# Seven block products for eight in the gate and up projections of the first token group, with smaller mixer buffers, an output projection fed by token range, and a shorter last reduction

## The chip, the cores and the metric

One core of a Trainium2 chip runs the whole kernel. The metric is the time of one execution on the device in microseconds (us). The engines have these names in all views: PE (matrix products, on TensorE), PEld (its weight loads), DVE (vector), ACT (scalar), POOL (GpSimd), SP (which here only issues DMAs). A DMA is issued by an engine's own instruction and runs on 16 DMA engines.

## The reference

One layer of an encoder over 1024 prompt tokens and 32 tokens of a running stream, all in fp32:

```python
h = x * (1 + sc1) + sh1                                   # conditioning from c @ w_ada
mq, mk, mv, mo, mi, mf, fq, fk, fv, ff, gu, gv = split(h @ w_in)
hm = mlstm(...)      # matrix memory, 4 heads       -> 256 columns
hf = fox(...)        # attention with forgetting, 8 heads -> 512 columns
hg = gmlp(...)       # spatial gate                 -> 256 columns
mix = concat([hm, hf, hg]) @ w_o
x = layer_norm(ALPHA * x + (1 + g1) * mix)
h = x * (1 + sc2) + sh2
y = (silu(h @ w_gate) * (h @ w_up)) @ w_down             # D_MODEL 1024, D_FF 2816
x = layer_norm(ALPHA * x + (1 + g2) * y)
```

## The kernel before

**Tiling.** Activations lie transposed, features on the 128 partitions, tokens along the free axis. The 1056 tokens are two groups: group 0 has 512, group 1 has 544 (two ranges of 272). D_FF is 22 tiles of 128 columns; a "tile j" below is the pair of gate and up columns number j, whose weights are `w_gu[j]`, 128 rows by 2048 (8 k-blocks of 128 for gate, 8 for up). Every fp32 product takes three passes of TensorE (`gemm`, L119 to L121): the weight and the activation are split into a rounded part (`whi`, `ah`) and a remainder (`wlo`, `al`), and the passes are hi by high, hi by low and lo by high. The split of a weight is one cast by ACT (L107) and one subtraction by DVE (L108), each on 1024 columns.

**Order of the program.** (1) Conditioning and the first projection; (2) the input projections, woven with the mixers of group 0; (3) `wo_mix(0)` loads the mixers' output of group 0 from DRAM (`dmix`) and splits it into the operand `ah`/`al`, `wo(0)` makes the output projection, range by range of 256 tokens, `ln1` normalizes; (4) the last projections of group 1; (5) the mixers of group 1 (`mixers`), at the same time the gate and up products (`up`) and the down products (`down`) of group 0: I call this the mixer stage, from about 470 to 900 us; (6) `wo(1)` and its normalization, and the rest of group 0's products; (7) the gate, up and down products of group 1; (8) the last normalization (`ln2`) and the stores.

**What sets the order.** The code is written through a tile framework whose scheduler places the instructions of each engine by priority and its own costs; the code's `weave` and `issue_after` are hints. Each engine then runs its own list strictly in order. Buffers are taken from pools of a fixed count, so an instruction also waits until the reader of an older buffer is done.

**The block scheme.** Group 1's tiles 3 to 20 are not made by `up` but by `sup`: of gate and up, each with two halves of 512 rows of k, and two token ranges, eight block products would be needed; `sup` forms sums of weight blocks and sums of operand blocks and makes seven products of 4 k-blocks by 272 tokens (84 matmuls). The operand's sums come once from `sup_operand`. Of the weights' sums, two come from DRAM: `sums()` stores a block of `w_gu` twice into `dp[j]` (a DMA of SP, L90), and a DMA of POOL (L1078) then adds two other blocks to it; two more are made by DVE out of the loaded blocks (L1132, L1133). Group 0 uses `up` for all 22 tiles: 2 times 8 k-blocks by 3 passes, 48 matmuls of 128x512.

**Last step.** `ln_sum` adds each finished row block m into `zs` (POOL, L899) and its square into `qs` (DVE, L901); `ln_stats` sums over the partitions by one product each with a matrix of 1/1024 (L908, L910).

## Time and profile before

| | |
|---|---|
| median of 3 runs | 1407.58 us (1405.99 to 1407.97) |
| the profiled execution | 1411.39 us, of which 1409.6 us are the span of its instructions |
| granted TensorE clock, mean over the span | 0.986 of full speed |
| PE busy | 1346.1 us (95%), 9437 matmuls |
| DVE / ACT / POOL busy | 999.4 (71%) / 656.3 (47%) / 261.1 us (19%) |
| DMA | 233.06 MB, a mean of 165 GB/s |

The page is read so: the shares are means over all stages, so the stages are looked at one by one, in rows that give for a stretch of time the busy time of each engine with its instruction count, the granted clock (1.00 is full speed), the DMA engines' busy share and the GB/s they moved. Rows of the timeline give start, duration, engine, line of the kernel, operation, and in brackets the idle time before it with what ended it. Matmuls are pipelined, so that the time a product costs is the distance from start to start, not its own duration.

### The profile page before, as it was taken

To read this page: it belongs to the slowest core of one execution; us is meant where nothing else is said; L and a number is where in the kernel's file an instruction comes from. 1 tells how busy PE (TensorE), PEld (TensorE's weight loads), DVE (VectorE), ACT (ScalarE), POOL (GpSimd) and SP (SyncE) were. 2 spreads that over 40 slices of the span, in tenths; PEclk is the share of its full clock that TensorE was granted. 3 is DMA by queue.
4 is the path that set the end of the run, shared out by engine and by line. 5 is a ranking of instruction groups with operands and counts; after the bars stand their busy time and mean duration, and the time that the engine had idled before them with its cause. 6 is when DMAs were issued, how large, how long until landed. Compare 5 with 4: busy or idle time off the path is not lost.

```text
span 1409.6 us, 25370 instructions
## 1 busy us (share of the span) xinstructions
PE 1346.1 (95%) x9437; PEld 1229.6 (87%) x9437; DVE 999.4 (71%) x2145; ACT 656.3 (47%) x1309; POOL 261.1 (19%) x297
## 2 busy tenths in 40 slices
PE   6999999999989899999999999999989999999995
PEld 4899989899979778888888878898989999999985
DVE  5548655578679657677767857577967887777666
ACT  3323244444445444545545354435744564636344
POOL 0103200042246500000000120073600000022031
PEclk9999999999999999999999999999999999999997
DMA  9754677575664864444444344675675768544221
GB/s 377 255 197 133 186 231 245 175 210 162 191 200 152 222 201 125 131 144 117 135 121 131 90 115 79 192 182 149 180 199 150 211 165 227 155 127 128 86 73 64
DMA packets 132915, 233.06 MB, mean 165 GB/s; under 512 B 22180, under 2 KB 79148, under 8 KB 129720
## 3 DMA queue, kind: packets, MB, share of 16 engines
q1 hardware_dynamic: 127624, 221.48, 51.3%
q0 software_dynamic: 5168, 9.96, 4.7%
q8 instruction: 74, 1.21, 0.4%
q14 instruction: 49, 0.40, 0.1%
HBM read 197.50 MB, written 53.81 MB: 178 GB/s over the span
## 4 chain that ended last, share of the span: by engine, by line
PE 73%; DMA 10%; DVE 8%; ACT 3%; issue 3%; POOL 2%; SPq 1%; ACTq 0%; DVEq 0%; POOLq 0%
PE up_g L121 4%; PE up_g L119 4%; PE up_g L120 4%; PE dn_g L119 4%; PE dn_g L120 4%; PE dn_g L121 4%; PE tm_g L312 2%; PE tm_g L313 2%; PE tm_g L311 2%; PE fm_g L119 2%; PE sup_g L119 2%; PE sup_g L121 2%; PE sup_g L120 2%; PE fm_g L120 2%; PE fox_t L773 2%
## 5 line engine op out<-in xcount | busy, mean ns | idle before, releaser
L119 PE MATMUL up_g<-mlstm_ah,up_whi 128*128 128x512 f32 x328 | 131.9, 403 | 3.7 <-DVE fm_qkl L396 2.5
L121 PE MATMUL up_g<-mlstm_ah,up_wlo 128*128 128x512 f32 x328 | 131.0, 399 | 0.0
L120 PE MATMUL up_g<-mlstm_al,up_whi 128*128 128x512 f32 x328 | 130.9, 399 | 0.0
L119 PE MATMUL fm_g<-start_h1h,fm_whi 128*128 128x256 f32 (+2 forms) x344 | 101.6, 303 | 9.5 <-DVE fm_qkl L396 4.8
L313 PE MATMUL tm_g<-tm_whi,start_h1l 128*128 128x256 f32 (+1 forms) x384 | 110.4, 288 | 0.0
L311 PE MATMUL tm_g<-tm_whi,start_h1h 128*128 128x256 f32 (+1 forms) x384 | 110.4, 289 | 0.0
L312 PE MATMUL tm_g<-tm_wlo,start_h1h 128*128 128x256 f32 (+1 forms) x384 | 110.1, 287 | 0.0
L120 PE MATMUL fm_g<-start_h1l,fm_whi 128*128 128x256 f32 (+2 forms) x344 | 101.5, 295 | 0.0
L121 PE MATMUL fm_g<-start_h1h,fm_wlo 128*128 128x256 f32 (+2 forms) x344 | 100.5, 293 | 0.0
L1126 ACT CAST sup_whi<-sup_raw 128x1024 fp32r<-128x1024 f32 x54 | 56.5, 1048 | 78.3 <-PE dn_u L120 37.2
L107 ACT CAST up_whi<-up_raw 128x1024 fp32r<-128x1024 f32 x50 | 52.3, 1046 | 64.2 <-PE up_g L120 29.5
L108 DVE TENSOR_TENSOR up_wlo<-up_raw,up_whi 128x1024 fp32r<-128x1024 f32 x50 | 63.2, 1264 | 25.8 <-ACT up_whi L107 24.9
L1127 DVE TENSOR_TENSOR sup_wlo<-sup_raw,sup_whi 128x1024 fp32r<-128x1024 f32 x54 | 68.6, 1275 | 15.4 <-ACT sup_whi L1126 15.1
L747 ACT ACTIVATE fox_p<-fox_s,fox_fmx 128x384 f32<-128x384 f32 (+2 forms) x96 | 55.3, 580 | 49.6 <-DVE fox_fmx L740 43.2
L119 PEld LDWEIGHTS fm_g<-start_h1h,fm_whi 128*128 128x128 f32 x344 | 65.2, 191 | 14.9 <-ACT start_h1h L232 8.2
L119 PEld LDWEIGHTS up_g<-mlstm_ah,up_whi 128*128 128x128 f32 x328 | 62.0, 189 | 17.6 <-DVE fm_qkl L396 3.0
L119 PE MATMUL dn_g<-up_acth,dn_whi 128*128 128x512 f32 (+2 forms) x200 | 73.7, 369 | 0.8 <-DVE mlstm_z L982 0.8
L120 PEld LDWEIGHTS up_g<-mlstm_al,up_whi 128*128 128x128 f32 x328 | 62.1, 189 | 14.1 <-issue 0.8
L121 PEld LDWEIGHTS up_g<-mlstm_ah,up_wlo 128*128 128x128 f32 x328 | 62.1, 189 | 13.9 <-issue 0.4
L312 PEld LDWEIGHTS tm_g<-tm_wlo,start_h1h 128*128 128x128 f32 x384 | 73.1, 190 | 0.7 <-issue 0.4
L313 PEld LDWEIGHTS tm_g<-tm_whi,start_h1l 128*128 128x128 f32 x384 | 73.0, 190 | 0.6 <-issue 0.4
L311 PEld LDWEIGHTS tm_g<-tm_whi,start_h1h 128*128 128x128 f32 x384 | 72.9, 190 | 0.8 <-issue 0.4
(618 smaller groups left out, 4561.2 us busy)
## 6 DMA issues: line engine op xcount, KB each, us to landing
up_raw<-w_gu SPq DMA_DIRECT2D x50, 512.0 KB
ada_late<-w_ada SPq DMA_DIRECT2D x16, 1024.0 KB
dn_raw<-w_dn SPq DMA_DIRECT2D x28, 512.0 KB
wo_raw<-w_o SPq DMA_DIRECT2D x24, 512.0 KB
sup_raw<-w_gu SPq DMA_DIRECT2D x20, 512.0 KB
start_dp<-w_gu SPq DMA_DIRECT2D x19, 512.0 KB
start_dp<-w_gu POOLq DMA_DIRECT2D x19, 512.0 KB, 7.6
sup_raw<-start_dp SPq DMA_DIRECT2D x18, 512.0 KB
```

Of the source, the lines that this page charges most:

```text
L107: nc.scalar.copy(hi[:, :w], raw[:, :w])
L108: (eng or nc.vector).tensor_tensor(lo[:, :w], raw[:, :w], f(hi[:, :w]), ALU.subtract)
L119: nc.tensor.matmul(ps, hi, xh(k), start=start and k == 0, stop=False, skip_group_check=more)
L120: nc.tensor.matmul(ps, hi, xl(k), start=False, stop=False, skip_group_check=more)
L121: nc.tensor.matmul(ps, lo, xh(k), start=False, stop=stop and k == n - 1, skip_group_check=more)
L311: nc.tensor.matmul(ps[:, :ncol], xh, hi, start=k == 0, stop=False)
L312: nc.tensor.matmul(ps[:, :ncol], xh, lo, start=False, stop=False)
L313: nc.tensor.matmul(ps[:, :ncol], xl, hi, start=False, stop=k == 7)
L747: nc.scalar.activation(pr[:, lo:hi], banks[x][:, :hi - lo], AF.Exp, bias=m, scale=-1.0 if hi == n else 1.0, accum_out=sums[:, x:x + 1])
L773: nc.tensor.transpose(ps[:, at + (y - first) * P:at + (y - first + 1) * P], probs[y][:, b * P:(b + 1) * P], self.ident)
L1126: nc.scalar.copy(h, x)
L1127: tt(l, x, f(h), ALU.subtract)
```

## The change

1. **Group 0, tiles 3 to 18, by `sup`.** `sup` gets the group as an argument; for group 0 it makes 84 matmuls of 128x256 where `up` made 48 of 128x512. `sup_operand0` builds the operand's sums from the residual `z` when tile 3 comes up: 8 ACT activations of 512 columns, then subtractions and splits by DVE and ACT, through one `sil` buffer. One sum overwrites a quarter of the operand in place, so `corner_store` saves that quarter in DRAM and `corner_load` brings it back after tile 18. For group 0 the two additions of weight blocks are made by POOL instead of DVE.
2. **`sums()` earlier.** The 19 stores and the 19 accumulating DMAs go from 900 to 1250 us to the mixer stage, two of them before it.
3. **Buffers.** The mixers' pool for group 1 has one `p` buffer and one `pth` buffer less, the mLSTM steps share buffers, `sil` has one buffer for two, and the row constants are split in two tiles.
4. **Softmax scaling.** `FP` is a table of which engine divides by the softmax sum in the attention of each group: for group 1 ACT does it instead of DVE (L755).
5. **`wo_mix(0)` by token range.** The eight loads of range 0 go ahead of those of range 1, and the first loads go ahead of the load of the residual.
6. **Conditioning units 20 to 23** go from the first tiles of group 0 to the projection loop before.
7. **Last reduction.** In the last half of group 1 the last two row blocks are not added to `zs` and `qs` but summed by TensorE as further products (`direct`, `more`); `ln2_end` normalizes in pieces of 4, 2, 1 and 1 blocks.

```diff
-FP = (0, 0)
+FP = (0, 1)
+MX1 = (1, 1, 1, 1, 3, 2)
+SJ0 = 3
+SE0 = 18
+SIL = 1
...
+    def sup_operand0(self):
...
+        (th, tl), (uh, ul) = self.T0
+        for k in range(4):
+            x, y = self.t(self.p2, [P, 544], F32, "sil", SIL)[:, :512], ys[k]
+            for q, o in ((k, x), (k + 4, y)):
+                nc.scalar.activation(o, self.z[0][:, q], AF.Identity, bias=self.modcol("sh2", q)[0],
+                                     scale=self.modcol("sc2", q)[0])
+            tt(y[:, b], y[:, b], x[:, b], ALU.subtract)
+            tt(x[:, b], x[:, a], x[:, b], ALU.subtract)
+            stt(x[:, a], x[:, a], -1.0, y[:, b], ALU.mult, ALU.subtract)
+            stt(y[:, a], x[:, a], -1.0, y[:, a], ALU.mult, ALU.subtract)
+            nc.scalar.copy(th[:, k], x)
+            tt(tl[:, k], x, f(th[:, k]), ALU.subtract)
+            nc.scalar.copy(uh[:, k], y[:, b])
+            tt(ul[:, k], y[:, b], f(uh[:, k]), ALU.subtract)
+        h, l = self.whole
+        for k in range(4):
+            nc.scalar.copy(h[:, k, b], ys[k][:, a])
+            tt(l[:, k, b], ys[k][:, a], f(h[:, k, b]), ALU.subtract)
...
-    def sup(self, j, act, pool):
+    def sup(self, c, j, act, pool):
...
-        tt(raw[0][:, lo], raw[0][:, lo], raw[1][:, hi], ALU.add)
-        tt(raw[0][:, hi], raw[0][:, hi], raw[0][:, lo], ALU.add)
+        add = (nc.vector if c else nc.gpsimd).tensor_tensor
+        add(raw[0][:, lo], raw[0][:, lo], raw[1][:, hi], ALU.add)
+        add(raw[0][:, hi], raw[0][:, hi], raw[0][:, lo], ALU.add)
...
+        if m in st.get("direct", ()):
+            st["more"].append((z[:, m, sl], sq))
+            return
...
-        self.wo_mix(0, self.KORDER[:6])
+        self.wo_mix(0, self.KORDER[:6], MM[0][:1])
...
-        self.wo_mix(0, self.KORDER[6:])
+        self.wo_mix(0, self.KORDER[6:], MM[0][:1])
+        self.wo_mix(0, self.KORDER, MM[0][1:])
...
-                weave(self.up(0, j, act, pa, FC[0]))
-                if j < 4:
-                    self.ada(20 + j, pa, "late", 1, self.pg, "g")
+                if j and self.nsum <= FF:
+                    self.sums(self.lastraw)
+                if j < SJ0:
+                    weave(self.up(0, j, act, pa, FC[0]))
+                else:
+                    if j == SJ0:
+                        weave(self.sup_operand0())
+                    weave(self.sup(0, j, act, pa))
```

How the change moves instructions is seen at three places in the engines' lists. In these rows stand the line, the operation, output and inputs with their buffer numbers, and the shape of the output; lines of the changed kernel are some higher (L123 to L125 are its three passes, L90 is its load, L94 its store).

SP, ahead of `wo(0)`. The operand of range 0 needs eight loads `wo_tmp`, one for each k-block. Before, six of them (4286 to 4306) are followed by six of range 1 (4310 to 4330), and only then by the last two of range 0 (5271, 5275):

```order
L90 DMA o_kT<-fm_qkr_5187 64x272
L90 DMA start_dqh_57<-fm_qkh_5226 128x272
L90 DMA start_dql_58<-fm_qkl_5227 128x272
L90 DMA o_kT<-fm_qkr_5228 64x272
L86 DMA wo_tmp_4318<-start_dmix_32_88 128x256
L86 DMA wo_tmp_4322<-start_dmix_32_88 128x256
L86 DMA wo_tmp_4326<-start_dmix_32_88 128x256
L86 DMA wo_tmp_4330<-start_dmix_32_88 128x256
L90 DMA start_dqh_57<-fm_qkh_5260 128x272
L90 DMA start_dql_58<-fm_qkl_5261 128x272
L90 DMA o_kT<-fm_qkr_5262 64x272
L86 DMA wo_tmp_5271<-start_dmix_32_88 128x256
```

Now the last two of range 0 (5242, 5246) come as the seventh and eighth load, ahead of all of range 1 (5250 and on):

```order
L94 DMA start_dqh_57<-fm_qkh_5122 128x272
L94 DMA start_dql_58<-fm_qkl_5123 128x272
L94 DMA o_kT<-fm_qkr_5124 64x272
L94 DMA start_dqh_57<-fm_qkh_5156 128x272
L94 DMA start_dql_58<-fm_qkl_5157 128x272
L94 DMA o_kT<-fm_qkr_5158 64x272
L94 DMA start_dqh_57<-fm_qkh_5197 128x272
L90 DMA wo_tmp_5242<-start_dmix_33_89 128x256
L90 DMA wo_tmp_5246<-start_dmix_33_89 128x256
L90 DMA wo_tmp_5250<-start_dmix_33_89 128x256
```

Six loads and the stores of two more projections no longer stand between the sixth and the seventh load of range 0.

PE, the first tiles of group 0 in the mixer stage. Before, the 24 products of a gate half and the 24 of an up half stand in one run each:

```order
L119 MATMUL up_g_8307<-mlstm_ah_4284,up_whi_8297 128x512
L120 MATMUL up_g_8307<-mlstm_al_4285,up_whi_8297 128x512
L121 MATMUL up_g_8307<-mlstm_ah_4284,up_wlo_8298 128x512
L119 MATMUL up_g_8332<-mlstm_ah_4284,up_whi_8303 128x512
L120 MATMUL up_g_8332<-mlstm_al_4285,up_whi_8303 128x512
```

Now the first block tile (bank `sup_g_8671` and `sup_g_8715`; `up_th`, `up_tl`, `up_uh`, `up_ul` are the operand's sums) is spread k-block by k-block between down products and attention:

```order
L871 MATMUL foxs_o_6514<-foxs_pth_6511,start_vs_158 64x32
L745 MATMUL fox_s_6547<-fox_k_1178_6532,fox_q_1179_6533 128x384
L745 MATMUL fox_s_6551<-fox_k_1178_6532,fox_q_1179_6533 128x256
L124 MATMUL sup_g_8671<-up_tl_8585,sup_whi_8658 128x256
L125 MATMUL sup_g_8671<-up_th_8584,sup_wlo_8659 128x256
L124 MATMUL sup_g_8715<-up_ul_8587,sup_whi_8662 128x256
L125 MATMUL sup_g_8715<-up_uh_8586,sup_wlo_8663 128x256
L123 MATMUL dn_g_8795<-up_acth_8362,dn_whi_8780 128x512
L124 MATMUL dn_g_8795<-up_actl_8363,dn_whi_8780 128x512
```

The products of tile 3 that need the operand's sums now stand ahead of down products that don't need them, in a list that PE runs in order.

POOL in the mixer stage. Before, it has three short instructions for each mLSTM step and nothing else:

```order
L554 MEMSET mlstm_mqb_6660 128x512
L559 MEMSET mlstm_mv_1230_6664 128x4
L570 TENSOR_TENSOR mlstm_mo_6667<-mlstm_mo_6667,start_rowp_175 128x256
L554 MEMSET mlstm_mqb_7098 128x512
L559 MEMSET mlstm_mv_1356_7102 128x4
L570 TENSOR_TENSOR mlstm_mo_7105<-mlstm_mo_7105,start_rowp_175 128x256
```

Now the two additions of each block tile (L1187, L1188) and the accumulating DMAs (L1091) stand in the same list:

```order
L574 TENSOR_TENSOR mlstm_mo_6746<-mlstm_mo_6746,start_rowp_176 128x256
L1187 TENSOR_TENSOR sup_raw_8646<-sup_raw_8646,sup_raw_8647 128x512
L1188 TENSOR_TENSOR sup_raw_8646<-sup_raw_8646 128x512
L1091 DMA start_dp_19_75<-w_gu 256x1x512
L1187 TENSOR_TENSOR sup_raw_8894<-sup_raw_8894,sup_raw_8895 128x512
L1188 TENSOR_TENSOR sup_raw_8894<-sup_raw_8894 128x512
L1091 DMA start_dp_20_76<-w_gu 256x1x512
L1091 DMA start_dp_21_77<-w_gu 256x1x512
L1187 TENSOR_TENSOR sup_raw_9030<-sup_raw_9030,sup_raw_9031 128x512
L1188 TENSOR_TENSOR sup_raw_9030<-sup_raw_9030 128x512
L558 MEMSET mlstm_mqb_7172 128x512
```

An accumulating DMA waits for its store to land, and additions of later tiles and memsets of later mLSTM steps are queued behind it.

181 lines of the change are left out of this document (124 added, 57 removed).

## The prediction

> **What bounds the kernel now.** I read the page first, then the busy times by stage, because the change adds work to three engines in one stage and takes some from a fourth.
>
> ```profile
> span 1409.6 us, 25370 instructions
> PE 1346.1 (95%) x9437; PEld 1229.6 (87%) x9437; DVE 999.4 (71%) x2145; ACT 656.3 (47%) x1309; POOL 261.1 (19%) x297
> q0 software_dynamic: 5168, 9.96, 4.7%
> 380.00:440.00 60.00, 52.85 (x412) 51.45 (x412) 47.85 (x66) 30.86 (x54) 34.84 (x31) 0.97 0.65 201
> 500.00:900.00 400.00, 397.75 (x2089) 328.56 (x2088) 274.16 (x565) 187.82 (x379) 17.51 (x26) 1.00 0.46 126
> 1000.00:1050.00 50.00, 46.43 (x356) 45.73 (x356) 41.08 (x76) 27.91 (x58) 13.54 (x15) 0.97 0.79 213
> 1050.00:1340.00 290.00, 289.15 (x2292) 287.96 (x2291) 224.83 (x398) 150.30 (x246) 29.51 (x26) 1.00 0.57 157
> ```
>
> The last four rows are stretches: length, then PE, PEld, DVE, ACT and POOL busy, the granted clock, the DMA share and GB/s. In the mixer stage (500 to 900) PE is busy 99.4% while DVE is at 69%. In group 1's block stage (1050 to 1340) DVE is at 78% and PE still at 99.7%. PE sets the pace in both, so a matmul less is time less as long as the others keep up. At 380 to 440, around the output projection of group 0, PE loses 7 us of 60.
>
> **Term 1: the products.** What a matmul costs is the distance of starts.
>
> ```profile
> 400.10 0.28 PE L119 MATMUL wo_g<-mlstm_ah,wo_whi 128*128 128x256 f32 x1
> 401.87 0.29 PE L119 MATMUL wo_g<-mlstm_ah,wo_whi 128*128 128x256 f32 x1
> 702.20 0.39 PE L121 MATMUL dn_g<-up_acth,dn_wlo 128*128 128x512 f32 x1
> 706.38 0.40 PE L121 MATMUL dn_g<-up_acth,dn_wlo 128*128 128x512 f32 x1
> ```
>
> These are first and last of two runs without a gap: 15 intervals of a 256-column product in 1.77 us, 0.118 each, and 18 intervals of a 512-column one in 4.18 us, 0.232 each. A tile of group 0 goes from 48 x 0.232 = 11.14 us to 84 x 0.118 = 9.91, a gain of 1.23; over 16 tiles **-20 us** (19.7, and 20.3 with unrounded spacings).
>
> A page speaks against this: the Trainium skill, "TensorE: Matmul & The Clock Gate", section "Back-to-back issue gap", has sustained spacings of 81 ns for 128 columns and 131 ns for 512. By a line between them, an estimate, 256 columns take 98 ns, a tile goes from 6.3 to 8.2 us, and 16 tiles cost 31 us more. This trace disagrees (118 and 232 ns); the same section's formula for an isolated product, columns / 2.4 + 2.5 ns, is what the rows follow.
>
> **Term 2: DVE, ACT and POOL in the mixer stage.** Durations, from the mixer stage and from group 1's block stage:
>
> ```profile
> L108 DVE TENSOR_TENSOR up_wlo<-up_raw,up_whi 128x1024 fp32r<-128x1024 f32 x38 | 46.8, 1232 | 21.6 <-ACT up_whi L107 20.7
> L1060 DVE TENSOR_TENSOR up_actl<-up_sil,up_acth 128x512 fp32r<-128x512 f32 x19 | 13.0, 684 | 0.9 <-ACT up_acth L1059 0.9
> L755 DVE TENSOR_SCALAR fox_p<-fox_p,fox_fsm 128x1024 f32<-128x1024 f32 x8 | 6.0, 753 | 0.2
> L755 DVE TENSOR_SCALAR fox_p<-fox_p,fox_fsm 128x640 f32<-128x640 f32 x8 | 4.4, 550 | 0.2
> L1127 DVE TENSOR_TENSOR sup_wlo<-sup_raw,sup_whi 128x1024 fp32r<-128x1024 f32 x50 | 62.4, 1253 | 11.9 <-ACT sup_whi L1126 11.8
> L1127 DVE TENSOR_TENSOR sup_w2l<-sup_raw,sup_w2h 128x512 fp32r<-128x512 f32 x17 | 11.9, 700 | 0.5
> L1177 DVE SCALAR_TENSOR_TENSOR sup_c<-sup_c,sup_sil 128x544 f32<-128x544 f32 x16 | 11.5, 721 | 0.1
> L1175 DVE TENSOR_TENSOR sup_sil<-sup_tmp,sup_sil 128x272 f32<-128x272 f32 x16 | 7.0, 437 | 2.2 <-ACT sup_sil L1174 2.2
> L1126 ACT CAST sup_whi<-sup_raw 128x1024 fp32r<-128x1024 f32 x50 | 52.3, 1049 | 76.8 <-PE dn_u L120 37.2 <-PE sup_u L120 13.6 <-PE sup_g L120 10.2
> L1153 ACT COPY sup_tmp<-sup_g 128x272 f32<-128x272 f32 x9 | 3.4, 382 | 2.7 <-PE sup_g L121 2.7
> ```
>
> Columns after the bar: sum in us, mean of one in ns, idle time before. DVE on a plain tile: two splits of 1.23 and three operations of 0.68, 4.5 us. On a block tile: three splits of 1.25, one of 0.70, two 512-wide at 0.72 and five narrow ones at 0.44, 8.1 us. Sixteen tiles add 57 us. `sup_operand0` adds, for each of four k, five narrow operations and one of 0.70, and four narrow ones more, 13 us. The softmax scaling leaves DVE: 32 operations between 0.55 and 0.75, 21 us. Sum for DVE **+49 us**. The stage then has, from 470 on, about 295 + 49 = 344 us of DVE in some 410, 84% where it had 69%. ACT gains one cast and a half (1.5), three copies (1.1) and split activations (0.4) a tile, 48 us, some 13 for the operand and 21 of the scaling: over 80 us, from 47% to about 68%. ACT is not the bound; its work is on the path only through DVE.
>
> What 84% costs PE, no row shows for this stage. From below: at 78% PE lost 0.85 of 290 us (0.3%), which gives 1 us. From above: in 1000 to 1050, with DVE at 82%, PE lost 3.57 of 50 us, 7%, which would give 29 us. The upper row is nearer in load, but most of its loss is one other thing:
>
> ```profile
> 1021.93 8.08 DMA sup_w2l<-start_dh
> 1034.88 0.39 PE L119 MATMUL up_u<-wo_ah,up_whi 128*128 128x272 f32 x1 [2.80 <-ACT up_whi L107]
> ```
>
> DVE's operand sums waited 8 us for a load from DRAM, and the weight splits behind them came 2.8 us late. Without it 0.7 of 50 us is left, 1.4%, which is 6 us over 410. To that comes the first block tile, which has such an operand chain of its own: counted over the changed lists between the first and the last product of tile 3, DVE has 44 us of these instructions and PE 35, so I take 9 us. Together **+15 us**, with 1 and 29 as ends.
>
> In this I count the POOL additions. Near ones are these:
>
> ```profile
> L1191 POOL TENSOR_TENSOR sup_z<-sup_raw,sup_z 128x1024 fp32r<-128x1024 f32 x2 | 4.8, 2378 | 62.6 <-ACT sup_z L1190 62.6
> 1342.57 2.37 POOL L1191 TENSOR_TENSOR sup_z<-sup_raw,sup_z 128x1024 fp32r<-128x1024 f32 x1 [5.03 <-ACT sup_z L1190]
> 1343.47 2.54 DVE L1127 TENSOR_TENSOR sup_wlo<-sup_raw,sup_whi 128x1024 fp32r<-128x1024 f32 x1 [1.35 <-ACT sup_whi L1126]
> L1078 POOL DMA_DIRECT2D start_dp<-w_gu x19 | 19.8, 1044 | 219.1 <-DMA start_dp<-w_gu 215.1 <-DVE wo_z L982 3.9
> start_dp<-w_gu POOLq DMA_DIRECT2D x19, 512.0 KB, 7.6
> ```
>
> An addition of 512 columns should take half of 2.38, 1.2 us; 32 are 38 us of an engine that was busy 17.5 of 400. A DVE split that began while POOL ran took 2.54 for 1.25, as if it had waited for POOL's end. The Trainium skill, "SBUF — State Buffer", section "SBUF: two separate sides", says that DVE operations with two SBUF inputs and POOL operations that read SBUF share one port pair, and that the later one is blocked for the whole instruction; the 2.54 agrees. By that rule alone, with each of 32 holds reaching PE, the sum below would be 32 us worse, an estimate. I take less, since a hold eats DVE's slack first: it is in the 6 us.
>
> **Term 3: the DMAs that move.** The accumulating DMAs are the software queue: 4.7% of 1409.6 us is 66 us of all 16 engines, 3.5 for each of 19. With their stores and 0.25 MB more for each block tile, the mixer stage's DMA share goes from 0.46 to about 0.7. Accumulates wait on POOL (215 us above), now ahead of additions and mLSTM memsets; the first two are issued before the stage and each is a tile or more ahead of its use, which hides 7.6 us of landing: 0, and up to 10 if that lead is gone. What leaves is the pressure at 1000 to 1050, where the 8 us load stood: -2.8 if it goes, 0 if not; I take **-1**.
>
> **Term 4: the output projection of group 0.**
>
> ```profile
> 388.97 2.58 DMA wo_tmp<-start_dmix
> 389.14 0.28 PE L121 MATMUL wo_g<-mlstm_ah,wo_wlo 128*128 128x256 f32 x1
> 391.45 1.98 SPq L86 DMA_DIRECT2D wo_tmp<-start_dmix  x4
> 394.34 1.01 PE L119 MATMUL wo_g<-mlstm_ah,wo_whi 128*128 128x256 f32 x3 [4.92 <-ACT mlstm_ah L943]
> ...
> 397.07 0.41 PE L120 MATMUL wo_g<-mlstm_al,wo_whi 128*128 128x256 f32 x1
> 397.28 0.41 PE L121 MATMUL wo_g<-mlstm_ah,wo_wlo 128*128 128x256 f32 x1
> ```
>
> The last k-blocks of range 0 are loaded behind six of range 1, each in need of a `tmp` buffer that ACT and DVE must empty; PE stands 4.92 us, and its next products start 0.21 apart until 397.7, at the lower clock. With the two loads ahead the stall goes and with it some 2 us of low clock; late next is `wo_raw`. Ends 0 and -7; I take **-5**.
>
> **Term 5: the tail.**
>
> ```profile
> 1392.84 2.59 DVE L901 TENSOR_TENSOR sup_qs<-sup_qs,dn_tmp 128x272 f32<-128x272 f32 x4
> 1393.01 0.43 ACT L898 ACTIVATE dn_tmp<-wo_z 128x272 f32<-128x272 f32 x1 [0.97 <-DVE wo_z L982]
> 1395.48 1.27 PE L910 MATMUL lnb_t<-sup_qs,start_onesm 128*128 128x272 f32 x2 [0.46 <-DVE sup_qs L901]
> 1402.35 4.14 ACT L1231 ACTIVATE wo_z<-wo_z,start_colp 128x272 f32<-128x272 f32 x8 [3.70 <-DVE wo_z L1230]
> ```
>
> Two of the last four additions (0.65 each) and two POOL additions go, the last square is there at 1393.44, so the last product could start 1.4 to 2 us sooner. Against it the first normalized piece is four blocks wide, so ACT starts about 1 us later after the statistics. **-1.5**, between -3 and +1.
>
> The smaller mixer buffers I cost at nothing alone: one `p` or `pth` less delays attention, which the other products of the stage cover; if they don't, it shows as part of term 2. The moved conditioning units are 32 small products and cost the same in either place.
>
> **Sum.** -20 + 15 - 1 - 5 - 1.5 = -12.5 on the profiled 1411.39, 1398.9. That execution is 3.8 above the median of 1407.58, so the forecast for the median is **1395 us**.
>
> **Rivals.** (a) *DVE paces the mixer stage.* One mechanism: POOL's additions hold DVE's splits, 32 x 1.2 = 38 us on 344 makes 382 of 410, 93%, and an engine at that share, whose inputs come from PE and ACT in turn, stalls PE. Price: 30 to 40 us in place of 15, hence 1410 to 1420, slower. It decides from a stall of 30.6 us on (28 to 30.6 is no change). For it: 7% lost at 82%. Against: 0.3% at 78%. (b) *DVE stays under PE* as in group 1: PE 99% or more and a first tile hidden by the down products between its k-blocks: 1 to 4 us of stall, 1381 to 1385. (c) *The transfers eat it.* A tile waits for its `dp` block, since an accumulate stands behind a store that has to land: 0.8 us a tile on top, 13 us, 1408, no change. For it: a share of 0.7 is what the stretches with gaps had (0.65, 0.79). (d) *Narrow products are no cheaper*, the page's rule: 51 us worse than my first term, 1446; the rows at 0.118 speak against.
>
> **Chances.** The forecast, 1388 to 1403: 0.48. (b), 1380 to 1388: 0.24. Between the forecast and no change: 0.06. (c) and what else ends within 0.2% of 1407.58 (1404.8 to 1410.4, about what can be told from no change): 0.09. (a): 0.12. (d): 0.01. So faster 0.78, same 0.09, slower 0.13. The range 1383 to 1409 leaves out about 0.05 below and 0.15 above.
>
> **What will show it.** In the profile after: `sup_g` products of group 0 at 0.118 from start to start (term 1); in 500 to 900, PE busy about 97% and DVE about 85% (term 2), with PE's idle time released by `sup_wlo`, most of it in tile 3; POOL additions of 1.2 us and some splits near 2.4; no gap of several us in `wo_g`; DMA at 0.7. PE at 99.5% in that stretch means (b); DVE above 90% with PE near 92% means (a); PE waiting for `sup_raw` from `start_dp` means (c). I am wrong above all if the first tile's chain is hidden, or if DVE's splits are held more often than I take.

## The result, and the profile after

The changed kernel is slower: 1419.01 us in the median against 1407.21 for the kernel before in the same comparison, a ratio of 1.007 with a 95% interval of [1.0045, 1.0096] (the two medians alone give 1.0084). The forecast was 1395. The profiled execution of the changed kernel took 1423.47 us, 12.1 more than that of before.

The page of the changed kernel, its first line and its busy times, and the rows by stretch (length, then PE, PEld, DVE, ACT and POOL busy, granted clock, DMA share, GB/s):

```profile
span 1421.6 us, 26984 instructions
PE 1336.7 (94%) x10021; PEld 1255.9 (88%) x10021; DVE 1039.2 (73%) x2227; ACT 731.0 (51%) x1457; POOL 302.2 (21%) x327
380.00:440.00 60.00, 55.18 (x442) 54.49 (x441) 48.76 (x65) 29.97 (x51) 35.39 (x33) 0.97 0.65 209
455.00:485.00 30.00, 14.99 (x115) 13.36 (x114) 15.81 (x35) 13.37 (x32) 20.69 (x24) 0.78 1.00 288
500.00:900.00 400.00, 379.89 (x2594) 345.88 (x2593) 315.52 (x648) 262.52 (x526) 77.01 (x73) 0.97 0.68 173
1000.00:1050.00 50.00, 46.52 (x373) 45.88 (x374) 47.15 (x93) 33.22 (x72) 21.50 (x22) 1.00 0.42 132
```

PE has less to do than before (1336.7 for 1346.1 us), and the span is 12 us longer. Two rows show where. In the mixer stage PE is busy 380 of 400 us where it was 398, with DVE at 79%, far from full. And at 455 to 485, a stretch that the prediction did not look at, PE is busy half the time and the DMA engines all of it. The same stretch of before:

```profile
455.00:485.00 30.00, 26.06 (x158) 21.73 (x156) 20.47 (x39) 17.15 (x37) 22.96 (x30) 0.94 0.70 198
```

To say where the 12 us came from I cut both traces at the first or last product of a kind, and split each stretch in two: the products' own time (for each matmul the distance to the next start, but no more than the median distance of its shape) and the rest, called stall. Stalls hold idle gaps and products that start further apart than the median of their shape, at a lower clock or for another reason. All numbers are us, from one profiled execution of each kernel; the first stall counts from the first product on:

| stretch, up to | length before, after | stall before, after | what it moves |
|---|---|---|---|
| the last `tm_g` (conditioning, input projections, group 0's mixers) | 372.1, 373.9 | 61.8, 63.0 | +1.8 |
| the first `lna_t` (output projection of group 0) | 66.2, 62.4 | 11.5, 7.8 | -3.8 |
| the first `up_g` (last projections of group 1) | 29.2, 47.0 | 4.7, 21.7 | **+17.8** |
| the first `up_u` (mixer stage) | 429.9, 432.3 | 28.5, 50.2 | **+2.4** (products -19.3, stall +21.7) |
| the first `dn_u` (output projection of group 1) | 81.9, 80.9 | 3.2, 2.0 | -1.0 |
| the first `sup_u` (rest of group 0, group 1's plain tiles) | 67.2, 61.3 | 10.8, 5.0 | -5.9 |
| the end | 363.1, 363.8 | | +0.7 (tail alone, from the last down product on, +1.1) |

Of the mixer stage's stall, 5.9 us are idle gaps before and 20.1 after, so 14 of the 21.7 us are time in which PE did nothing. The border between the two bold rows moved, too: in the changed kernel 68 products of the conditioning stand ahead of the first `up_g`, before none. Over a fixed 100 us from the first `lna_t` on, the stall is 19.0 before and 29.7 after.

**Ahead of the mixer stage.** The chain that ended last, in the stretch 440 to 490 of the changed kernel (start, length, what), and the same place in the timeline:

```profile
456.86 10.69 DMA start_dqh<-fm_qkh
469.80 12.85 DMA start_dql<-fm_qkl
482.74 0.51 DVE fm_qkl L400
483.29 0.79 PE L123 MATMUL up_g<-mlstm_ah,up_whi 128*128 128x512 f32 x1 [4.56 <-DVE fm_qkl L400]
483.88 0.63 PE L124 MATMUL up_g<-mlstm_al,up_whi 128*128 128x512 f32 x1
...
488.15 0.63 PE L125 MATMUL up_g<-mlstm_ah,up_wlo 128*128 128x512 f32 x1
488.58 0.53 PE L123 MATMUL up_g<-mlstm_ah,up_whi 128*128 128x512 f32 x1
```

The projections store their results (`fm_qkh`, `fm_qkl`) in DRAM, 136 KB at a time, from a small ring of buffers. Two such stores took 10.7 and 12.9 us, the ring was full, and PE stood. Then its products started 0.43 apart until 488.6.

**In the mixer stage.** What PE waited for between 500 and 900 us (total, times, longest), first before, then after:

```profile
PE fox_t L773 <- ACT mlstm_mixs L662: 1.4, 1, 1.4
PE fox_s L737 <- DMA fox_qp<-start_dql: 0.5, 1, 0.5
```

```profile
PE fox_s L744 <- DMA fox_k<-start_dqh: 13.0, 4, 7.8
PE fox_o L788 <- DVE fox_ptl L786: 3.3, 2, 2.5
PE sup_g L123 <- ACT sup_tmp L1213: 0.7, 1, 0.7
```

Most of PE's idle time now lies at the start of an attention head (`fox_s`, the scores), and none of it is a wait for weight splits. The longest of these waits in the chain:

```profile
787.82 13.48 DMA start_dp<-w_gu
801.85 1.04 POOL start_dp L1091
802.89 0.54 POOL mlstm_mqb L558
803.45 5.41 DMA mlstm_mqb<-start_dmqk
808.88 8.67 DMA fox_k<-start_dqh
```

A store of `sums()` took 13.5 us to land. POOL held its accumulating DMA for it, and with that the memset of an mLSTM step; the load into that tile stood on SP ahead of the load of the next head's keys.

### The profile page after: what moved, and what is told of

It is laid out like the page before. It is cut to its first block, busy times and chain, and to the rows that moved or that the text cites. A ratio compares the mean times of both kernels' runs of the same rounds, so it can differ in the third digit from the quotient of the medians.

```text
span 1421.6 us, 26984 instructions
## 1 busy us (share of the span) xinstructions
PE 1336.7 (94%) x10021; PEld 1255.9 (88%) x10021; DVE 1039.2 (73%) x2227; ACT 731.0 (51%) x1457; POOL 302.2 (21%) x327
## 3 DMA queue, kind: packets, MB, share of 16 engines
q8 instruction: 79, 1.29, 0.4%
## 4 chain that ended last, share of the span: by engine, by line
PE 46%; DMA 8%; DVE 6%; ACT 4%; issue 2%; POOL 1%; SPq 0%; POOLq 0%; ACTq 0%; DVEq 0%
PE sup_g L123 5%; PE sup_g L125 4%; PE sup_g L124 4%; PE dn_g L123 3%; PE dn_g L125 3%; PE dn_g L124 3%; PE sup_u L124 2%; PE sup_u L123 2%; PE sup_u L125 2%; DMA fox_k<-start_dqh 2%; PE dn_u L123 1%; PE dn_u L124 1%; PE dn_u L125 1%; PE fox_t L781 1%; PE wo_g L125 1%
## 5 line engine op out<-in xcount | busy, mean ns | idle before, releaser
L1180 ACT CAST sup_whi<-sup_raw 128x1024 fp32r<-128x1024 f32 x102 | 106.7, 1047 | 96.9 <-PE dn_u L124 43.1
L1181 DVE TENSOR_TENSOR sup_wlo<-sup_raw,sup_whi 128x1024 fp32r<-128x1024 f32 x102 | 127.4, 1252 | 32.2 <-ACT sup_whi L1180 31.4
L123 PE MATMUL fm_g<-start_h1h,fm_whi 128*128 128x256 f32 (+2 forms) x344 | 101.5, 302 | 17.6 <-DVE fm_qkl L400 12.9
L125 PE MATMUL fm_g<-start_h1h,fm_wlo 128*128 128x256 f32 (+2 forms) x344 | 101.0, 294 | 0.0
L123 PE MATMUL dn_g<-sup_acth,dn_whi 128*128 128x512 f32 (+2 forms) x248 | 85.6, 345 | 1.6 <-DVE mlstm_z L995 1.2
L123 PEld LDWEIGHTS fm_g<-start_h1h,fm_whi 128*128 128x128 f32 x344 | 65.1, 191 | 23.0 <-ACT lna_tmp L1014 10.6
L125 PE MATMUL dn_g<-sup_acth,dn_wlo 128*128 128x512 f32 (+2 forms) x248 | 85.3, 344 | 0.0
L124 PE MATMUL dn_g<-sup_actl,dn_whi 128*128 128x512 f32 (+2 forms) x248 | 84.5, 341 | 0.0
L124 PEld LDWEIGHTS fm_g<-start_h1l,fm_whi 128*128 128x128 f32 x344 | 65.9, 192 | 2.5 <-issue 0.8
L401 POOL TENSOR_TENSOR fm_qkr<-fm_qkh,fm_qkl 128x256 f32<-128x256 f32 (+1 forms) x32 | 33.7, 1055 | 161.2 <-DVE fm_qkl L400 145.3
L125 PEld LDWEIGHTS fm_g<-start_h1h,fm_wlo 128*128 128x128 f32 x344 | 65.7, 191 | 1.1 <-issue 0.4
L786 DVE TENSOR_TENSOR fox_ptl<-fox_t,fox_pth 128x512 fp32r<-128x512 f32 (+2 forms) x88 | 50.6, 584 | 17.7 <-ACT fox_pth L785 17.4
L785 ACT CAST fox_pth<-fox_t 128x512 fp32r<-128x512 f32 (+2 forms) x88 | 43.2, 510 | 36.2 <-PE fox_t L781 36.0
```

The source lines that it names most:

```text
L123: nc.tensor.matmul(ps, hi, xh(k), start=start and k == 0, stop=False, skip_group_check=more)
L124: nc.tensor.matmul(ps, hi, xl(k), start=False, stop=False, skip_group_check=more)
L125: nc.tensor.matmul(ps, lo, xh(k), start=False, stop=stop and k == n - 1, skip_group_check=more)
L401: nc.gpsimd.tensor_tensor(kr[:, :n], f(hi[:, :n]), f(lo[:, :n]), ALU.add)
L785: nc.scalar.copy(ph[:, :at], ps[:, :at])
L786: nc.vector.tensor_tensor(pl[:, :at], ps[:, :at], f(ph[:, :at]), ALU.subtract)
```

## Experiments

Each ratio is to the kernel before in the same comparison, with its 95% interval. "Stall" is that of the table above; the mixer stage's is meant unless said.

### What stops the projections ahead of the stage

The conditioning units moved alone, in the kernel before:

```diff
+            self.ada(16 + h, pq, "late", 2, self.pt, "t")
-                if j < 4:
-                    self.ada(20 + j, pa, "late", 1, self.pg, "g")
```

> The kernel before with one change: conditioning units 20 to 23 are made in the projection loop ahead of the mixers instead of beside the first tiles of group 0. Theory A (their 4 MB of loads delay the stores that free the projections' buffers): the first up product starts 10 us or more later than before and the mixer stage wins back at most 3, so 7 to 12 us slower. Rival (the two early block sums and the earlier weights make that delay): the first up product starts 2 to 4 us later, the whole within 2 us of before.

The new places of `sums()` alone, in the kernel before:

```diff
+        self.sums()
+        self.sums()
-                self.sums()
+                if j and self.nsum <= FF:
+                    self.sums(self.lastraw)
```

> The kernel before with the block sums at the changed kernel's places: two ahead of the mixers, the rest beside group 0's tiles. Theory S: a gap of about 10 us ahead of the mixers, 5 to 15 us more stalls in the mixer stage, 5 to 7 us back at 1000 to 1050: 8 to 18 us slower than before. Theory D: within 4 us of before, since PE had slack for them.

The changed kernel without the two sums ahead of the stage, so that each sum comes a tile later; and with all sums far earlier, from the ninth item of the first mixers' stage on:

```diff
-        self.sums()
-        self.sums()
-                if j and self.nsum <= FF:
+                if self.nsum <= FF:
```

> The changed kernel with the two block sums that stood ahead of the mixers started one tile later each, beside group 0's first tiles. Theory S (the early stores and accumulates delay the stores that free the last projections' buffers): the gaps of 10.6 and 4.9 us at 458 and 478 shrink to 5 us together as in the kernel before, and the whole is 8 to 14 us faster than the changed kernel. Rival (the change's other orders make those gaps): they stay above 12 us together, and the time is within 4 us of the changed kernel.

```diff
+            if n >= 8 and self.nsum <= FF:
+                self.sums(self.lastraw)
```

> The changed kernel with all block sums' stores and accumulates moved into the first mixers' stage (about 200 to 370 us), one for each step of that stage. Theory S2 (they only hurt where they meet the last projections' stores and the four conditioning loads, at 455 to 480): the stretch from the first normalization to the first up product falls from 47 to about 33 us; the mixer stage of group 1 stays at some 430 us; if the first stage has room, 10 to 17 us faster than the changed kernel. Rival (POOL and the queues have no room earlier either): the first stage grows by 10 us or more and nothing is won.

| run | ratio | projections: length, stall | mixer stage's stall |
|---|---|---|---|
| before / after | 1 / 1.007 | 29, 4.7 / 47, 21.7 | 28.5 / 50.2 |
| `b_ada` | 0.9966 [0.9951, 0.9981] | 32, 7.3 | 22.0 |
| `b_sums` | 1.007 [1.0043, 1.0097] | 33, 8.0 | 41.6 |
| `a_late` | 1.012 [1.0088, 1.0152] | 34, 9.1 | 71.7 |
| `a_sums0` | 1.0267 [1.0247, 1.0288] | 32, 7.2 | 47.8 |

The stretch 455 to 485 of `b_ada`, `b_sums` and `a_late`:

```profile
455.00:485.00 30.00, 26.19 (x162) 22.39 (x161) 18.59 (x41) 18.37 (x40) 24.86 (x30) 0.94 0.68 199
```

```profile
455.00:485.00 30.00, 24.88 (x155) 20.44 (x156) 20.10 (x36) 17.24 (x38) 23.04 (x28) 1.00 0.87 250
```

```profile
455.00:485.00 30.00, 25.48 (x170) 21.81 (x168) 20.32 (x44) 18.03 (x39) 24.73 (x26) 0.94 0.92 262
```

Each move alone costs the projections some 3 us; in the changed kernel, with both, they lose 17. At DMA shares of 0.68, 0.87 and 0.92 the longest `fm_qkl` store in the chain of that stretch took 4.3, 7.4 and 5.5 us; at 1.00 they took over 10. By the trace four stores of `sums()` were issued ahead of the first `up_g` in the changed kernel, not the two of the code's place, and three in `a_late`. That the early sums are one half of the loss is shown: with one fewer the stretch is 34 us (`a_late`), without any 32 (`a_nodp`, below). That the conditioning is the other half is the likely reading, not shown, since no run takes it alone out of the changed kernel. One rival is left: in `b_ada`, `a_late` and `a_nodp` the scheduler put 32 conditioning products ahead of the first `up_g`, in the changed kernel 68, so PE's order differs, too.

The fixed 100 us from the first `lna_t` on don't depend on that border. Their stall is 19.0 before, 15.2 in `b_ada`, 21.9 in `b_sums` and 29.7 after (31.0 without the block scheme, `a_nosup` below). So the changed kernel loses more there than the two moves alone add up to, and the block scheme is not what does it.

`a_late` frees the stretch and still loses: its stall in the mixer stage is 21 us larger than the changed kernel's. `a_sums0` shows the other side: with the transfers in the first mixers' stage, the time up to the last `tm_g` went from 374 to 425 us. Neither place was free.

### What the block products cost in the stage

Four kernels: with and without the block scheme in group 0, and with and without the DMAs that form the weights' sums. Without the scheme, `up` makes group 0's tiles (and the corner is neither saved nor loaded); without the DMAs, `raw[1]` comes straight from `w_gu`.

```diff
-                if j < SJ0:
+                if j < FF:
```

> The changed kernel with group 0's tiles 3 to 18 made by plain up again (48 products of 512 columns); everything else of the change stays, the block sums' DMAs at their new places too. Theory D (DVE, ACT and POOL of the block scheme make the stalls): the mixer stage has few stalls, 430 us at most, total about as the changed kernel or faster by up to 5 us. Theory K (the key buffer and the DMAs make them): the waits for fox_k stay at 8 us or more in sum, and with the 20 us of products back the total is 8 to 20 us slower than the changed kernel.

```diff
-                self.store(self.dp[i], blocks(i)[:, 2:3].to_broadcast([P, 2, 512]))
+            pass
-            self.nc.gpsimd.dma_start(self.dp[i - 1], blocks(i - 1)[:, 0:4:3], accum_op=ALU.add)
+            pass
-        self.load(raw[1], self.dp[j].rearrange("p b n -> p (b n)"))
+        self.load(raw[1], self.d["w_gu"][j][:, 1024:])
```

> The changed kernel without the stores and accumulates of the block sums: each block tile loads 512 KB of w_gu in place of the sum, so the products have wrong weights but the same shapes. Theory S (the sums' transfers and POOL's and SP's queues behind them make the stalls, ahead of the mixers and in the mixer stage): 20 to 30 us faster than the changed kernel, PE busy 99% in 500 to 900. Theory D (DVE, ACT and POOL's additions make the mixer stage's stalls): only the gap ahead of the mixers goes, 8 to 14 us faster, PE stays near 95% in 500 to 900.

Both edits together:

> The changed kernel with neither group 0's block products nor the block sums' stores and accumulates (group 1's block tiles load w_gu in place of the sums, so their products have wrong weights and the same shapes). What is left of the change in the mixer stage is the smaller buffers, the shared mLSTM buffers and the scaling by ACT. Theory Q (attention's chain through the smaller buffers makes the stage's stalls): stalls of about 40 us in the mixer stage as with the sums, 10 us or more slower than before. Theory X (the sums and the block scheme each make them, by themselves): stalls of 22 to 28 us as in the kernel before, and 0 to 8 us faster than before.

| stall in the mixer stage; ratio | with the sums' DMAs | without |
|---|---|---|
| block products in group 0 | 50.2; 1.007 | 50.3; 0.9945 [0.9922, 0.9969] |
| plain products in group 0 | 44.3; 1.0212 [1.0185, 1.0238] | 22.9; 0.9944 [0.9924, 0.9965] |

The mixer stage of the two kernels without sums, block products first:

```profile
500.00:900.00 400.00, 380.73 (x2601) 346.32 (x2600) 316.34 (x647) 262.45 (x526) 59.42 (x56) 0.98 0.52 141
```

```profile
500.00:900.00 400.00, 394.52 (x2040) 327.56 (x2038) 254.08 (x523) 214.48 (x411) 16.57 (x26) 1.00 0.46 123
```

In the right column the scheme is worth nothing: 0.9945 and 0.9944. It saves 19 us of products and adds 50.3 - 22.9 = 27 us of stall in a stage that no block sum disturbs, at a DMA share of 0.52. The stage is 8 us longer with it, and the output projection of group 1 behind it 5 us shorter (80.9 for 86.2). Term 2 of the prediction had these 27 us at 15. The sums alone add 44.3 - 22.9 = 21 us to a plain stage, and nothing to a block stage: the two costs do not add up, as if both used up one slack. (In the plain kernel with the sums, 11 us of the loss lie behind the stage, in an output projection of group 1 of 92 us.) What the sums cost the block kernel lies elsewhere: its projections are 32 us long without them for 47.

What that slack is, I read from the order of the products; this is a reading, not shown. Between the last scores of one head and the first of the next stand products of `up`, `sup` or `down`, which cover the softmax and the loads. For the seven changes of head, their own time and PE's wait behind it:

```
before        6.5/0.1 6.5/0.0 7.7/0.0 6.5/0.0 6.3/0.1 7.4/0.0 7.4/0.0
after         4.9/1.3 5.8/0.2 6.8/0.0 4.3/2.0 11.2/0.0 4.6/2.4 9.6/8.0
a_nodp        4.9/2.7 5.8/0.4 6.8/0.0 4.3/1.8 11.2/0.0 4.6/3.1 8.6/3.7
a_nosup_nodp  9.2/0.0 6.5/0.0 8.6/0.0 8.6/0.0 9.2/0.0 9.3/0.0 9.1/1.6
```

Before, every head has over 6 us of cover. With block products it is 4.3 to 5 at three changes, and PE waits at each of them. The waits in these rows add up to 13.9 us after and 11.7 in `a_nodp`, so they leave some 8 of the 21.7 us and 17 of the 27 to other places; and the longest, 8.0, came at 9.6 us of cover. The scheme also raises the busy time of DVE in the stage from 272 to 336 us and of ACT from 228 to 280 (`a_nosup_nodp` and `a_nodp`), which no run separates from the cover.

### What an engine's work is worth there

The POOL additions given to DVE, and the softmax scaling given back to DVE:

```diff
-        add = (nc.vector if c else nc.gpsimd).tensor_tensor
+        add = nc.vector.tensor_tensor
```

> The changed kernel with the two additions of weight blocks of group 0's tiles by DVE (0.71 us each) instead of POOL (1.29 us each). Theory P (POOL's additions hold DVE's splits, and stand behind accumulates in POOL's list): the stalls of the mixer stage fall by 5 to 10 us. Theory D (DVE itself is too full): they grow by 10 us, from 23 us more of DVE work. Theory Q (attention's chain through one key buffer and fewer p and pth buffers sets the stalls): within 4 us.

```diff
-FP = (0, 1)
+FP = (0, 0)
```

> The changed kernel with group 1's softmax scaling by DVE again (21 us of DVE work back, the same off ACT). Theory D: the mixer stage 5 to 10 us longer, since DVE goes from 79% to 84%. Theory Q: the stage is the same within 4 us, or shorter, since ACT's part of attention's chain (exponential, scaling, transposed copy) gets shorter.

`a_add_dve` measured 1.0136 [1.0108, 1.0165] and `a_fp0` 1.0165 [1.0143, 1.0188]. Stalls are 61.9 and 60.2, against 50.2. The 32 additions on DVE, by line, operation, shape and count (busy, mean ns), and other operations of DVE, in `a_add_dve` and then, with the additions on POOL, in the changed kernel:

```profile
L1187 DVE TENSOR_TENSOR sup_raw<-sup_raw,sup_raw 128x512 f32<-128x512 f32 x16 | 11.3, 704 | 5.3 <-DMA sup_raw<-start_dp 5.2
L1188 DVE TENSOR_TENSOR sup_raw<-sup_raw 128x512 f32<-128x512 f32 x16 | 10.9, 682 | 0.1
L1239 DVE SCALAR_TENSOR_TENSOR sup_c<-sup_c,sup_sil 128x512 f32<-128x512 f32 x15 | 10.2, 680 | 0.0
```

```profile
L1187 POOL TENSOR_TENSOR sup_raw<-sup_raw,sup_raw 128x512 f32<-128x512 f32 x16 | 22.4, 1399 | 117.3 <-DVE sup_wlo L1181 96.0 <-DVE sup_c L1228 14.5 <-DMA sup_raw<-start_dp 6.1
L1181 DVE TENSOR_TENSOR sup_wlo<-sup_raw,sup_whi 128x1024 fp32r<-128x1024 f32 x48 | 58.9, 1228 | 18.5 <-ACT sup_whi L1180 18.1
L1239 DVE SCALAR_TENSOR_TENSOR sup_c<-sup_c,sup_sil 128x512 f32<-128x512 f32 x16 | 11.7, 732 | 0.1
```

The additions are 22.2 us of work, but DVE's busy time in the stage rose by only 4.0 (333.6 to 337.6 us), while the stall rose by 11.7. The scaling raised it by 17.5 (to 351.1), and the stall by 10. So these runs give no single price for a microsecond of DVE, and `a_k1two` and `a_bufs` below, which add no work, raise the stall by 8, too. Nor does DVE's share alone set it: from 568.6 to 604.2 us of the changed kernel DVE is busy 32.09 of 35.60 us (90%) and PE 35.56, from 760 to 830 DVE 51.25 of 70 (73%) and PE 62.12. What stands is that both choices of the change, POOL for the additions and ACT for the scaling, are the faster ones in this kernel (1.007 against 1.0136 and 1.0165).

A part of the 22.2 us comes back because POOL's additions hold DVE. The Trainium skill, "SBUF — State Buffer", section "SBUF: two separate sides", has a DVE operation with two inputs in SBUF and a POOL operation that reads SBUF block each other: the later one waits for the whole of the other. The trace agrees. A sum of two narrow columns, 0.15 us in the median, began while POOL added and ended with it:

```profile
592.44 1.67 POOL L1187 TENSOR_TENSOR sup_raw<-sup_raw,sup_raw 128x512 f32<-128x512 f32 x1 [8.99 <-DVE sup_wlo L1181]
592.88 1.25 DVE L757 TENSOR_TENSOR fox_fsm<-fox_fsm 128x1 f32<-128x1 f32 x1
```

In the changed kernel's stage 19 DVE operations took over 0.1 us longer than the median of their kind, 13.0 us in all, each of them beside a POOL instruction; in `a_add_dve` they are 7 and 3.3 us, before 7 and 3.1. `fox_ptl`, which has one input in PSUM, kept its 0.68 us in all 13 cases beside an addition. The 48 splits with their mean of 1.228 show nothing of it: POOL's addition waits for a split (the 96.0 us in the row above), and no split ran beside one.

### Buffers

The mixers' pool of group 1 lost more than the text ahead of the prediction says: the key buffer `k1` (the first number of `MX1`) went from two to one as well. One key buffer alone, and the whole shrunk pool, each in the kernel before:

```diff
-        self.mixer_pool("mx1", s4, (2, 1, 1, 1), side="right")
+        self.mixer_pool("mx1", s4, (1, 1, 1, 1), side="right")
```

> The kernel before with one change: group 1's attention has one buffer for the keys (k1) where it had two. Theory K (the key load of the next head can only start once the last head's products are done, and PE waits for it): fox_s waits for fox_k some 2 to 8 us at each of the later heads, 10 to 20 us slower than before, with a lower granted clock behind each gap. Theory D (the block scheme's DVE and POOL work is what stalls the mixer stage): within 3 us of before, since the other products of the stage cover the load.

```diff
+        self.mixer_pool("mx1", s4, (1, 1, 1, 1, 3, 2), side="right")
```

> The kernel before with the smaller buffers of group 1's attention: one for the keys, three for the softmax rows (p) in place of four, two for their transposes (pth) in place of three. Theory B (the smaller buffers cost on their own): 5 to 12 us slower than before, fox_s and fox_o waiting. Theories S and D: within 4 us of before, as the one key buffer alone was.

And buffers given back in the changed kernel: `k1` for one `p`; `k1` alone, and `k1`, `p` and `pth` together, where the room comes from letting the remainders of the operand sums share the rounded parts' memory; and the last of these without the sums' DMAs:

```diff
-MX1 = (1, 1, 1, 1, 3, 2)
+MX1 = (2, 1, 1, 1, 2, 2)
```

> The changed kernel with two key buffers again; for the room, the softmax rows (p) have two buffers instead of three. Theory K: the waits of fox_s for fox_k go (13.6 us in five), with the low clock behind them 10 to 18 us faster than the changed kernel, unless the missing p buffer takes some back. Theory D: the stalls only move to fox_ptl and sup_wlo; within 5 us of the changed kernel.

```diff
-MX1 = (1, 1, 1, 1, 3, 2)
+MX1 = (2, 1, 1, 1, 3, 2)
+        self.T0 = ([self.t(self.pT, [P, 4, 512], F32R, "th", 1)] * 2,
+                   [self.t(self.pT, [P, 4, 256], F32R, "uh", 1)] * 2)
```

> The changed kernel with two key buffers; p and pth stay at three and two. For the room, the low parts of the operand's sums share the high parts' buffers (same instructions, wrong values). Theory Q by the key buffer alone: the waits of fox_s for fox_k (13.6 us) go and the mixer stage gets 10 to 18 us shorter. Theory X: within 5 us of the changed kernel.

```diff
-MX1 = (1, 1, 1, 1, 3, 2)
+MX1 = (2, 1, 1, 1, 4, 3)
```

> As the run with two key buffers, and with four p and three pth buffers as in the kernel before (low parts of the operand's sums share the high parts' buffers: wrong values, same instructions). Theory Q: the mixer stage's stalls fall from 50 to about 30 us, 15 to 22 us faster than the changed kernel. Theory X: 5 us faster at most, since the sums' transfers and the block scheme's chain remain.

> As the run with all three buffer counts of before, and without the block sums' stores and accumulates (wrong values twice over, same products). Theory Q: the mixer stage's stalls are 25 us or less and the whole is 25 us or more faster than before. Theory D (DVE and ACT of the block scheme set the stage): stalls stay at 40 us or more, 8 to 12 us faster than before as without the sums alone.

| run | ratio | mixer stage: length, stall |
|---|---|---|
| `b_k1` | 1.0011 [0.9995, 1.0027] | 433, 31.8 |
| `b_bufs` | 1.0084 [1.0061, 1.0106] | 433, 31.4 |
| `a_k1two_p2` | 1.0127 [1.0103, 1.0151] | 432, 47.9 |
| `a_k1two` | 1.0133 [1.0101, 1.0165] | 443, 58.3 |
| `a_bufs` | 1.0153 [1.0107, 1.0198] | 441, 58.4 |
| `a_bufs_nodp` | 0.9979 [0.9962, 0.9996] | 435, 51.2 |

The shrunk pool's stage has some 3 us more of stall, and these three buffers given back bring nothing: it is not they. (The shared mLSTM buffers and the single `sil` stay in `a_nosup_nodp`, too, at a stall of 22.9.) What PE waited for in the stage with all three back (`a_bufs`):

```profile
PE fox_o L788 <- DMA fox_v<-start_dv: 5.5, 2, 3.2
PE fox_s L744 <- DMA fox_qp<-start_dql: 3.4, 2, 2.3
PE fox_s L745 <- DMA fox_k<-start_dql: 3.0, 2, 2.5
PE fox_s L745 <- DMA fox_k<-start_dfs: 2.8, 2, 1.8
```

The 13.0 us on one load of keys are gone, and waits on the values and on the other inputs of the scores stand in their place. `b_bufs` is a warning of another kind: its loss of 0.8% lies in the output projection of group 1, 92 us for 82, where nothing was changed. A pool's size can move the scheduler's order in places far from the pool. The changed kernel does not have this loss (80.9 us there).

### Parts of the change without the rest

Moving the conditioning units pays by itself (`b_ada`, 0.9966): its mixer stage is 423 us for 430, at 3 us more in the projections. So does a lighter start of group 1. In the kernel before, first the moved units with `wo_mix(0)` by token range and the sums begun at tile 12 of group 0; then the moved units with the sums where they were, but none beside group 1's three plain tiles; then that with `wo_mix(0)` by token range:

```diff
+                if j > 11:
+                    self.sums(self.lastraw)
```

> The kernel before with three parts of the change that do not touch the block scheme: the conditioning units ahead of the mixers, the output projection of group 0 fed by token range, and seven of the block sums made beside group 0's last tiles in the mixer stage. From the parts so far: -5 us (conditioning, measured), -4 us (output projection, from the stretch in the changed kernel's trace), -4 us (the load that waited at 1021, if enough sums leave that place): 8 to 13 us faster than before. Rival (each sum in the mixer stage costs what it saves): 3 to 8 us faster.

```diff
-                if self.nsum <= FF:
+                if j >= SJ and self.nsum <= FF:
                     self.sums()
```

> A version from what the runs showed: the kernel before with the conditioning units 20 to 23 ahead of the mixers (4 to 5 us, measured) and no block sum issued beside group 1's tiles 0 to 2, where PE stood 2 to 3 us behind an 8 us load at 1021; no block scheme for group 0. If the sums are what fills that place: 7 to 11 us faster than before. If that load is slow by itself: 4 to 5 us faster, as with the conditioning alone.

```diff
-        self.wo_mix(0, self.KORDER[6:])
+        self.wo_mix(0, self.KORDER[6:], MM[0][:1])
+        self.wo_mix(0, self.KORDER, MM[0][1:])
```

> As the other run of this call, and the output projection of group 0 fed by token range. The residual's loads still stand ahead of the first operand loads here (they do not in the changed kernel). If the order of the eight loads alone matters: 3 to 4 us faster than the other run. If the residual's loads ahead of them are what PE waits for: within 2 us of the other run.

`b_ada_wo_s` measured 0.998 [0.9964, 0.9996], `c_ada_skip` 0.9931 [0.9908, 0.9954], `c_ada_wo_skip` **0.9909 [0.9885, 0.9933]** (1400.20 us against 1411.83), the fastest of all. The stretch at 1000 to 1050 in `c_ada_skip`:

```profile
1000.00:1050.00 50.00, 49.03 (x388) 48.71 (x388) 38.17 (x73) 29.36 (x59) 6.45 (x7) 1.00 0.55 153
```

The DMA share is 0.55 where it was 0.79, and PE 49.0 where it was 46.4. That stretch up to the first `sup_u` is 64 us long, against 67 before and 69 in `b_ada`. The range order shortened the output projection from 67 to 64 us, in line with the -3.8 of the whole change, and the gap ahead of the late loads' products is 1.3 us where it was 5.0. But the two ratios' intervals overlap, so its share of the total is not told from none. Sums from tile 12 on (`b_ada_wo_s`) kept the 70 us.

## Why the prediction was wrong

**Term 1, right.** Narrow products start 0.118 apart in the changed kernel:

```profile
600.63 0.28 PE L124 MATMUL sup_g<-mlstm_al,sup_whi 128*128 128x256 f32 x1
...
601.81 0.28 PE L125 MATMUL sup_g<-mlstm_ah,sup_wlo 128*128 128x256 f32 x1
```

That is ten intervals in 1.18 us, and the stage's products fell by 19.3 us for the 20 forecast. (The formula that the prediction says the rows follow gives 109 and 216 ns; the rows, 118 and 232, are 8% above it.)

**Term 2, the size inside its ends, the working wrong.** I took 15 and gave 1 and 29; it was 21.7. The sum for DVE was near: 40 us more busy in the stage (293.5 to 333.6) for 49. The 21.7 is a net figure: the scheme adds 27 by the four kernels above, and the conditioning units, moved alone, take 6.5 off the stage and put 2.6 on the projections (`b_ada`), where I had taken nothing. But I looked for the loss in weight splits late from a full DVE and in tile 3's operand chain, with PE at 97% and DVE at 85%. It was 95% and 79%, and the longest waits are at the heads. The step that failed is the choice of the rows at 1000 to 1050 and 1050 to 1340 as bounds: both are stages without attention. DVE at 78% went with a loss of 0.3% there and DVE at 79% with 5% here, in a stage in which PE, DVE, ACT and DRAM follow one another head by head. Rival (a) named the right price (1410 to 1420) by a mechanism that came small: POOL's additions did hold DVE, but the holds add up to 13 us where it took 38, nearly all on other operations than the weight splits, and DVE stays at 79% over the stage where it took 93%. (The prediction's "28 to 30.6 is no change" doesn't fit its own band of 1404.8 to 1410.4, which is a stall of 24.7 to 30.3.)

**Term 3, the step that turned the sign.** I costed the early accumulates at 0, up to 10 if their lead were gone, and the moved conditioning units at "the same in either place" (they are 72 products in the trace of before, not 32, and their weights are loads of 4 MB). I asked whether the sums would be there in time, and not whom they would delay. In the changed kernel the projections lose 17.8 us, the largest piece of the 24.5 us between the forecast difference (-12.5) and the sum of the stretches (+12.0). I had looked at each part alone, and the runs that did one part alone found 3 us each; that they meet is shown for the sums and likely for the conditioning, as said above. Rival (c) had the cause, transfers, but put it on `sup_raw` waiting for `dp`: in the changed kernel's list of PE's waits no such row stands. The relief at 1000 to 1050, for which I took -1, was larger, -5.9.

**Term 4, right in size, not in its sign to see:** -3.8 for -5. The gap of 4.92 us is gone, but "no gap of several us in `wo_g`" did not come:

```profile
400.40 0.55 PE L123 MATMUL wo_g<-mlstm_ah,wo_whi 128*128 128x256 f32 x1 [4.41 <-ACT wo_qs L903]
```

ACT's casts ahead of that had waited for `wo_raw`, which the prediction names as late next. PE's idle time in the stretch fell from 7.1 to 4.8 us, so that the size is right owes something to luck.

**Term 5, wrong by 2.6 us:** -1.5 forecast, +1.1 measured (19.1 us from the last down product to the end, 18.0 before). In the tail of the changed kernel:

```profile
1404.88 0.73 PE L921 MATMUL lnb_t<-sup_zs,start_onesm 128*128 128x272 f32 x2 [2.17 <-POOL sup_zs L910]
1406.82 1.08 PE L924 MATMUL lnb_t<-dn_tmp,start_onesm 128*128 128x272 f32 x4
1407.72 2.28 DVE L1291 TENSOR_TENSOR wo_z<-wo_z,sup_zs 128x1088 f32<-128x1088 f32 x3 [2.05 <-ACT sup_zs L927]
1409.92 0.49 DVE L928 SCALAR_TENSOR_TENSOR sup_qs<-lnb_t,start_epsa,sup_qs 128x272 f32<-128x272 f32 x1
1414.12 4.14 ACT L1293 ACTIVATE wo_z<-wo_z,start_colp 128x272 f32<-128x272 f32 x8 [2.79 <-DVE wo_z L1291]
```

The last down product started at 1402.4 (1391.6 before), so the sums end 5.5 us behind it and 5.15 before. Here the step failed: I had let the last product start 1.4 to 2 us sooner and put the products that replace the additions at nothing. The row blocks summed by TensorE take 1.08 us for each of the two sums (the row of 1406.82 is one), which takes what the additions gave back. Behind that I had allowed 1 us more for the wide first piece; it was 0.6: the variance's step (L928) stands behind subtractions of 2.28 us together in DVE's list, and the final activations begin 11.7 us after the last product, 10.75 before.

**The buffers, right for this kernel:** costed at nothing alone; alone (`b_bufs`) they are 3 us of the stage, and 0.8% in all by an output projection that did not grow in the changed kernel.

**What stays open.** That the block scheme by itself adds 27 us of stall is shown; what makes it is not. That the loss of cover between heads is the cause is a reading of the order, not shown: no run restored the cover alone, and `a_bufs` speaks partly against it (3.3 to 6.4 us of cover, waits of 0 to 1.3 there, and the stall as high elsewhere in the stage). DVE's and ACT's longer chains are the rival, untested alone. Why buffers do not help is open too, and so is whether the conditioning's loads or the order of its products meet the early sums.

## What to carry over

Where PE waits for nothing in a stage, ask what covers each chain of other engines beside it: here cheaper products brought 27 us of stall for 19 saved, and a chain left uncovered is the likely reason. A busy share taken from another stage did not bound this one. When transfers are moved, add up the DMA share of the stretch that they move into, with everything else that moves there, and name the small stores that will stand behind them. Try the parts alone before the whole: two of seven, with the sums thinned where DMA was busiest, took 0.9% off a time to which all seven added 0.7%.

## What the runs showed of the hardware

- With the DMA share at 1.00, stores of 136 KB took 10.7 and 12.9 us; at 0.68, 0.87 and 0.92 the longest in the chain of that stretch took 4.3, 7.4 and 5.5. In the mixer stage, at 0.68, a 512 KB store from DRAM to DRAM took 13.5 us, and through POOL's list and SP's its lateness reached PE as a gap of 8 us.
- After a gap of 4.6 us PE's 512-column products started 0.43 apart for 5.3 us (483.29 to 488.58), against 0.232 later. The Trainium skill, "TensorE: Matmul & The Clock Gate", section "Wait — 56ns, not 53.3ns?", gives 426.7 ns for 512 columns on a cold array, and the trace agrees. So this gap cost some 2.5 us beyond its own length (12 intervals, 5.29 us, less 12 x 0.232).
- An addition of 512 columns took POOL 1.29 us in the median (means 1.33 and 1.40) where I had halved the 1024-column row to 1.2, and DVE 0.68 to 0.70. Beside POOL's instructions DVE operations lost 13.0 us in the stage, 3.3 with the additions on DVE.
